# A decoder trunk in split fp32r: the block form at pairs 5, 7 to 19, and a scheduler told of a longer load latency

## The chip, the core and the metric

The kernel runs on one core of one Trainium2 chip. The metric is the device time of one execution in microseconds; the median of three runs counts. Times inside an execution are microseconds from the start of the profiled span. TensorE's matmuls are called PE, its weight loads PEld, VectorE DVE, ScalarE ACT, GpSimd POOL; SP issues most of the loads.

## What is computed

Two layers over 512 tokens of width 1024, then a final norm. Cut to what matters:

```python
for l in range(DEPTH):                                   # DEPTH = 2
    mod = silu(c) @ w_ada[l] + b_ada[l]
    sh1, sc1, g1, sh2, sc2, g2 = split(mod, 6)
    h = modulate(rmsnorm(x, norm1[l]), sh1, sc1)
    proj = h @ w_in[l]                                   # retention, gates and pooling branches
    ...
    x = x + g1 * (merged @ w_out[l])
    h2 = modulate(rmsnorm(x, norm2[l]), sh2, sc2)
    gate, up = split(h2 @ w_ffn_in[l], 2)                # 1024 x 5632: 22 pairs of 128 columns
    x = x + g2 * ((silu(gate) * up) @ w_ffn_out[l])      # 2816 x 1024
return rmsnorm(x, final_norm)
```

## The kernel before

**Split products.** Every weight and activation tile is split into a rounded part (hi) and a rest (lo), both fp32r. A product is three matmuls: hi·hi, lo·hi, hi·lo (mm3). Activations lie transposed, as 8 tiles (k-tiles) of 128 features by 512 tokens.

**Weights.** They stream in chunks of 8 blocks of 128x128 (512 KB, tensor wst). For a chunk, prep loads it into one of three raw tiles (SP), rounds it to hi (a cast, on ACT or DVE) and makes lo by a subtraction (DVE or POOL). For chunks for which is_added says so, ACT writes -hi into lo instead, and a DMA issued by POOL adds the weights to it from memory. Eleven w tiles hold hi and lo. ahead() prepares a chunk and the two behind it (LOOK). The three raw tiles also take the rows of w_ada, 96 loads in all: each is multiplied with silu(c) and summed by one DVE instruction (mod_tile).

**The FFN.** A pair i is a tile of gate columns and one of up columns, so 16 weight blocks, two chunks. In the plain form each is 8 k-tiles times 3 matmuls of 512 columns, 48 a pair; then SiLU on ACT, a product on DVE, and a split (cast and subtraction). In the block form (seven) the two tiles, the two halves of k and the two halves of the tokens are a 2x2 product of blocks done with seven products instead of eight: 7 products times 4 k-tiles times 3 matmuls, 84 matmuls of 256 columns. It needs sums of the activations (sums, the x tiles, made once a layer), sums of its weights (four instructions of 256 columns for each chunk, more casts and subtractions, seven_prep), four PSUM banks instead of two, and five additions on DVE behind the matmuls before SiLU. A block's two chunks are also prepared in the plain form by ahead() of the plain pair before it; nothing reads those. SEVEN (line 66) lists the pairs that are done as blocks: 4, 6, ... 20 in both layers.

The FFN runs in two halves, pairs 0 to 10 and 11 to 21 (FF_CUTS); behind each, ffn_out multiplies the hidden tiles and adds the result to x (close). The first ffn_out of a layer starts with output tile 0, over hidden tiles 0 to 10 in order, so pair 10's is read last. The first two pairs are partly made by first_tiles, and the sums are made while pairs 1 to 3 run.

**What sets the order.** All work is recorded first (Recorder). PE executes in program order. The other engines' order is set by a list scheduler (order) with costs of its own: each operation has a due time, counted back from the matmul that needs it, and LATENCY (line 217) of the engine is added from an operation's end to what depends on it. For "sync", the loads by SP, it is 1.6 us behind the cost of the transfer. It enters the due times, the moment at which a load's readers count as ready, and the moment at which buffers come free. The scheduler also chooses between ACT and DVE or DVE and POOL for some operations, by which would be done sooner.

**The start.** For each of the 8 k-tiles, two rows of w_ada and one chunk of w_in are loaded into the three raw tiles, the modulated k-tile of h is made, and 24 matmuls are issued into eight banks (start). Loads of the rotary tables (x from rot) stand in SP's queue between them.

In the trace nearly every instruction has line 421, that of the call which emits it (below: emit); so one goes by tiles: h are activations, x sums (and other pairs of tiles), w weights, r rows kept (hidden tiles, sums of weights), t temporaries, ps PSUM banks, xall the residual stream.

Of the kernel before, what the change touches and what calls it, by code (L numbers as in the profile page):

```python
# [17 lines left out]
DEPTH = 2  # L18
# [8 lines left out]
FT = FF // P  # L27
# [35 lines left out]
STAT_TILES = {"out": 4, "ffn_out": 3}  # L63
STAT_AT = 2

SEVEN = [set(range(4, FT, 2)), set(range(4, FT, 2))]
HALF_KT = KT // 2


# [144 lines left out]
TABLES = (AF.Sigmoid, AF.Silu, AF.Abs_reciprocal_sqrt)  # L214
TABLE_US = 1.28
LANDS = 6.0
LATENCY = {"tensor": 0.19, "vector": 0.05, "scalar": 0.05, "gpsimd": 0.05, "sync": 1.6}


class Recorder:  # L220
    def __init__(self):
        self.ops, self.tags, self.urgent = [], {}, False
        for e in LATENCY:
            setattr(self, e, Engine(self, (e,)))
# [28 lines left out]
    def deadlines(self):  # L253
# [13 lines left out]
        for op in reversed(self.ops):  # L267
# [3 lines left out]
            for o in op.after + reuse.get(op, []):  # L271
                if o.n > op.n:
                    op.due = min(op.due, o.due - LATENCY[e] - op.cost(e) - (LANDS if op.added else 0.0))
            if op.urgent and (e == "sync" or op.table is AF.Silu):
                op.due = op.n - 1e6

    def order(self):
# [4 lines left out]
        self.deadlines()  # L282
        free = {e: 0.7 for e in LATENCY}
        free["sync"] = 1.7
# [10 lines left out]
        taken, warm, late = set(), 6.83, 0.0  # L295
        ready = {e: [] for e in LATENCY}
        pe = [o for o in self.ops if o.engines[0] == "tensor"]
        pe_at = 0

        def arrive(o):  # L300
            pe = o.engines[0] == "tensor"
            o.at = max([done[b] + (0.0 if pe and b.ran == "tensor" else LATENCY[b.ran]) for b in o.before] or [0.0])
            for e in o.engines:
# [22 lines left out]
        while len(out) < len(self.ops):  # L326
            best = None
            for e in LATENCY:
                if e == "tensor":
# [103 lines left out]
def trunk(ctx, tc, xT, cin, wada, vecs, wst, rot, trid, icnt, out):  # L433
# [424 lines left out]
    for l in range(DEPTH):  # L858
# [222 lines left out]
        for f, (i0, i1) in enumerate(zip(FF_CUTS, FF_CUTS[1:])):  # L1081
            hid = []
            for i in range(i0, i1):
                if i in SEVEN[l]:
                    hid.append(seven(i))
# [114 lines left out]
```

## Time and profile before

| | |
|---|---|
| runs, us | 1560.45, 1557.97, 1560.12; median 1560.12 |
| the profiled execution, us | 1553.07, its span 1551.3 |
| mean granted TensorE clock in it | 0.992 |
| POOL's DMAs (w from wst) | 129 of 512 KB, 7.6 us median from issue to landing |
| SP's loads of w_ada (raw from wada) | 96 of 512 KB, 4.9 us median |

The profiled execution is a run of its own: its parts are compared with its own span. A row of the page's groups gives line, engine, operation, out<-in with partitions x elements and the count, then busy time, mean ns of one, and the engine's idle time ahead of them. A row of a timeline gives start and duration in us, engine, line, operation, operands, count, and in brackets the engine's idle time just before, with the instruction that ended it. A row of the windows gives the stretch, its length, busy time and count of PE, PEld, DVE, ACT and POOL, and then the granted clock, the share of DMA and GB/s.

### The profile page before, as it was taken

What the parts mean: (1) busy time and instruction counts of PE and PEld (TensorE: products, weight loads), DVE (VectorE), ACT (ScalarE), POOL (GpSimd) and SP (SyncE); (2) the same over time, 40 slices, a digit from 0 to 9 for tenths busy, and PEclk for the clock granted to TensorE, in tenths of its full rate; (3) what the DMA queues carried; (4) which work ended last, traced back from release to release, by engine and by line L of the source; (5) the groups of instructions that cost most, each with busy time, mean ns of one, the idle gap of its engine ahead of it and who ended that gap; (6) DMA issues with size and microseconds to landing.
All of it is one profiled execution on the core that took longest, in us unless ns stands there. A gap on an engine that the chain in (4) does not pass through costs nothing. (4 is left out here: it accounts for less than half of the span.)

```text
span 1551.3 us, 20752 instructions
## 1 busy us (share of the span) xinstructions
PE 1507.6 (97%) x7950; PEld 1290.2 (83%) x7950; DVE 1022.4 (66%) x1677; ACT 669.8 (43%) x949; POOL 292.2 (19%) x279
## 2 busy tenths in 40 slices
PE   7999999999999999999999999999999999999997
PEld 5788878888888878998898888888889887889987
DVE  7887693366568866888376767435647887368833
ACT  2387552223455321343267766323227544234432
POOL 0023150011133310122011322211111513001101
PEclk9999999999999999999999999999999999999999
DMA  7758637789784486556687865768897646534553
GB/s 251 250 154 214 154 84 216 203 240 269 170 217 155 158 245 190 163 182 217 198 206 162 209 157 124 206 181 234 242 233 179 200 164 197 155 123 150 174 139 82
DMA packets 83367, 288.89 MB, mean 186 GB/s; under 512 B 9282, under 2 KB 11586, under 8 KB 83267
## 3 DMA queue, kind: packets, MB, share of 16 engines
q1 hardware_dynamic: 64690, 219.92, 42.6%
q0 software_dynamic: 18576, 67.64, 24.3%
q8 instruction: 62, 1.02, 0.3%
q14 instruction: 39, 0.31, 0.1%
HBM read 285.43 MB, written 2.10 MB: 185 GB/s over the span
## 5 line engine op out<-in xcount | busy, mean ns | idle before, releaser
L421 PE MATMUL ps<-h,w 128*128 128x512 f32 (+1 forms) x3864 | 781.7, 360 | 8.2 <-DVE h L421 4.4
L421 PEld LDWEIGHTS ps<-h,w 128*128 128x128 f32 x3864 | 650.6, 189 | 123.4 <-ACT h L421 4.8
L421 PE MATMUL ps<-r,w 128*128 128x512 f32 (+1 forms) x2430 | 479.9, 357 | 7.4 <-DVE r L421 4.5
L421 PEld LDWEIGHTS ps<-r,w 128*128 128x128 f32 x2430 | 402.8, 188 | 78.5 <-DVE r L421 6.7
L421 ACT CAST w<-raw 128x1024 fp32r<-128x1024 f32 (+2 forms) x192 | 194.5, 1014 | 350.9 <-DMA raw<-wst 228.0
L421 POOL DMA_DIRECT2D w<-wst x129 | 115.4, 894 | 734.9 <-ACT w L421 673.4
L421 DVE TENSOR_TENSOR w<-raw,w 128x1024 fp32r<-128x1024 f32 (+2 forms) x158 | 194.2, 1234 | 88.5 <-PE ps L421 45.1
L421 ACT ACTIVATE w<-w 128x1024 fp32r<-128x1024 f32 x129 | 136.6, 1059 | 176.9 <-PE ps L421 60.8
L421 DVE SCALAR_TENSOR_TENSOR raw<-raw,cact 128x1024 f32<-128x1024 f32 x96 | 123.9, 1293 | 121.6 <-DMA raw<-wada 116.0
L421 DVE CAST w<-raw 128x1024 fp32r<-128x1024 f32 (+2 forms) x108 | 77.4, 717 | 106.3 <-DMA raw<-wst 58.7
L421 PE MATMUL ps<-x,w 128*128 128x256 f32 x864 | 109.3, 281 | 8.0 <-DVE w L421 4.2
L421 PEld LDWEIGHTS ps<-x,w 128*128 128x128 f32 x864 | 104.5, 190 | 9.6 <-DVE w L421 5.1
L421 POOL TENSOR_TENSOR r<-t,r 128x512 fp32r<-128x512 f32 x41 | 67.5, 1655 | 157.5 <-ACT r L421 144.9
L421 ACT CAST r<-t 128x512 fp32r<-128x512 f32 (+1 forms) x114 | 69.9, 618 | 47.6 <-DVE t L421 40.9
L421 PE MATMUL ps<-w,h 128*128 128x512 f32 x384 | 90.3, 395 | 0.0
L421 PEld LDWEIGHTS ps<-w,h 128*128 128x128 f32 x384 | 72.0, 188 | 17.7 <-ACT r L421 0.3
L421 DVE SCALAR_TENSOR_TENSOR xall<-ps,mod,xall 128x512 f32<-128x512 f32 (+1 forms) x62 | 38.7, 629 | 65.9 <-PE ps L421 65.8
L421 ACT ACTIVATE t<-ps 128x512 f32<-128x512 f32 x74 | 43.7, 592 | 50.4 <-PE ps L421 50.3
L421 DVE TENSOR_TENSOR w<-r,w 128x512 fp32r<-128x512 f32 x70 | 51.1, 737 | 12.4 <-ACT w L421 5.5
L421 ACT ACTIVATE t<-xall 128x256 f32<-128x256 f32 (+1 forms) x46 | 22.3, 497 | 82.3 <-DVE xall L421 79.1
L421 DVE TENSOR_TENSOR t<-ps,t 128x512 f32<-128x512 f32 x78 | 53.2, 684 | 6.3 <-PE ps L421 5.0
L421 ACT COPY t<-ps 32x512 f32<-32x512 f32 (+2 forms) x90 | 48.0, 535 | 21.4 <-DVE t L421 11.9
(95 smaller groups left out, 1020.8 us busy)
## 6 DMA issues: line engine op xcount, KB each, us to landing
raw<-wst SPq DMA_DIRECT2D x299, 512.0 KB, 4.6
w<-wst POOLq DMA_DIRECT2D x129, 512.0 KB, 7.6
raw<-wada SPq DMA_DIRECT2D x96, 512.0 KB, 4.9
x<-rot SPq DMA_DIRECT2D x32, 256.0 KB, 7.5
xall<-xT SPq DMA_DIRECT2D x4, 512.0 KB, 6.1
out<-t SPq DMA_DIRECT2D x7, 256.0 KB, 2.3
out<-t SPq DMA_DIRECT2D x2, 128.0 KB, 2.0
tri<-trid SPq DMA_DIRECT2D x1, 128.0 KB
```

What stands on the lines that cost most here:

```text
L421: getattr(eng, method)(*[real(a) for a in args], **{k: real(v) for k, v in kw.items()})
```

## The change

Two numbers change. The block form is taken by pairs 5, 7, ... 19 of both layers, 8 each instead of 9: pairs 4, 6, ... 20 are plain now, and the odd ones from 5 to 19 are blocks. The latency of SP's loads, for the scheduler, is 2.6 us instead of 1.6.

```diff
-SEVEN = [set(range(4, FT, 2)), set(range(4, FT, 2))]
+SEVEN = [set(range(5, FT - 1, 2))] * DEPTH
...
-LATENCY = {"tensor": 0.19, "vector": 0.05, "scalar": 0.05, "gpsimd": 0.05, "sync": 1.6}
+LATENCY = {"tensor": 0.19, "vector": 0.05, "scalar": 0.05, "gpsimd": 0.05, "sync": 2.6}
```

PE's program order changes only by the pairs' forms. On the other engines the scheduler sets a new order, and three places of it are shown. The numbers in names only tell tiles of one build apart.

**First place: DVE in the start,** behind the rounding of h's second k-tile (h_271 before, h_250 now). raw from wada is multiplied with cact; raw_257 and raw_224 are the third chunk of w_in. Before:

```order
39 L421 TENSOR_SCALAR h_271<-t_260,mod_0_150 128x512
40 L421 SCALAR_TENSOR_TENSOR raw_204,mod_0_150<-raw_204,cact_73 128x1024
41 L421 CAST w_286<-raw_257 128x1024
42 L421 SCALAR_TENSOR_TENSOR h_291<-t_260,mod_0_150,h_271 128x512
43 L421 SCALAR_TENSOR_TENSOR raw_235,mod_0_150<-raw_235,cact_73 128x1024
```

Now:

```order
41 L421 TENSOR_SCALAR h_250<-t_236,mod_0_150 128x512
42 L421 CAST w_269<-raw_224 128x1024
43 L421 SCALAR_TENSOR_TENSOR raw_182,mod_0_150<-raw_182,cact_73 128x1024
44 L421 TENSOR_TENSOR w_288<-raw_224,w_269 128x1024
45 L421 SCALAR_TENSOR_TENSOR raw_194,mod_0_150<-raw_194,cact_73 128x1024
46 L421 SCALAR_TENSOR_TENSOR h_307<-t_236,mod_0_150,h_250 128x512
```

The cast of the chunk moved ahead of the product with the first of the two w_ada rows, and the lo part of h moved behind both products. On SP, four loads of rotary tables stand right behind this chunk's load now, where one stood between the next two w_ada loads.

**Second place: ACT in layer 0's first FFN pairs.** ps_3511 is pair 0's gate tile and ps_3526 pair 1's; x tiles are the sums, r_3906, r_3901 and r_3980 sums of pair 4's weights. Before:

```order
280 L421 ACT_TABLE_LOAD
281 L421 ACTIVATE t_3930<-ps_3511 128x512
282 L421 CAST w_3915<-r_3901 128x512
283 L421 CAST w_3942<-raw_3870 128x768
284 L421 CAST r_3949<-t_3930 128x512
285 L421 CAST x_3973<-t_3889 128x512
286 L421 CAST w_3988<-r_3980 128x512
287 L421 CAST x_3996<-t_3928 128x512
288 L421 ACTIVATE t_4003<-ps_3526 128x512
```

Now:

```order
273 L421 ACT_TABLE_LOAD
274 L421 ACTIVATE t_3900<-ps_3511 128x512
275 L421 CAST x_3917<-t_3882 128x512
276 L421 CAST r_3921<-t_3900 128x512
277 L421 CAST x_3933<-t_3894 128x512
278 L421 ACTIVATE t_3946<-ps_3526 128x512
```

The casts of the block's weights are gone from between the two SiLUs (ACTIVATE t<-ps).

**Third place: the end of layer 0's first FFN half.** On ACT, t_4817 is the block at pair 10 before; raw tiles are chunks of the ffn_out that follows:

```order
336 L421 CAST r_4797<-t_4762 128x512
337 L421 CAST w_4806<-raw_4756 128x1024
338 L421 CAST w_4830<-raw_4781 128x1024
339 L421 ACTIVATE t_4817<-t_4817 128x512
340 L421 ACTIVATE w_4852<-w_4830 128x1024
```

On ACT now, t_4666 is the block at pair 9 and t_4732 the plain pair 10 (ps_4685 its gate tile):

```order
321 L421 ACTIVATE t_4666<-t_4666 128x512
322 L421 CAST w_4717<-raw_4670 128x1024
323 L421 ACTIVATE t_4732<-ps_4685 128x512
324 L421 CAST w_4741<-raw_4697 128x1024
325 L421 ACTIVATE w_4749<-w_4741 128x1024
```

And on DVE now, up to pair 10's split (raw_4738 is a row of layer 1's w_ada, ps_4730 pair 10's up tile):

```order
573 L421 SCALAR_TENSOR_TENSOR raw_4738,mod_0_4770<-raw_4738,cact_73 128x1024
574 L421 TENSOR_TENSOR t_4732<-ps_4730,t_4732 128x512
575 L421 CAST r_4785<-t_4732 128x512
576 L421 TENSOR_TENSOR r_4791<-t_4732,r_4785 128x512
```

Pair 10's SiLU now reads a bank directly and has one cast of a loaded chunk ahead of it instead of two.

## The prediction

> **What bounds the kernel.** First comes the first part of the page, the busy shares, and the last long piece of the chain of work that ended last.
>
> ```profile
> span 1551.3 us, 20752 instructions
> PE 1507.6 (97%) x7950; PEld 1290.2 (83%) x7950; DVE 1022.4 (66%) x1677; ACT 669.8 (43%) x949; POOL 292.2 (19%) x279
> ...
> 1309.20 231.97 PE ps L421 x1312
> ```
>
> PE is busy for 1507.6 of 1551.3 us, and from 1309 us on the end hangs on an unbroken run of matmuls. So the time is PE's work plus the 43.7 us in which it stands still. What another engine saves counts only where PE waits for it. The second view is therefore PE's timeline, with its idle time in brackets; these are its twelve longest waits between 70 and 1500 us.
>
> ```profile
> 226.16 0.51 PE L421 MATMUL ps<-r,w 128*128 128x512 f32 x1 [1.81 <-DVE r L421]
> 228.14 1.52 PE L421 MATMUL ps<-r,w 128*128 128x512 f32 x3 [1.47 <-ACT r L421]
> ...
> 426.38 0.99 PE L421 MATMUL ps<-acc,ones 128*128 128x256 f32 x2 [2.02 <-DVE acc L421]
> ...
> 474.21 4.62 PE L421 MATMUL ps<-x,w 128*128 128x256 f32 x24 [2.96 <-ACT t L421]
> ...
> 545.79 0.86 PE L421 MATMUL ps<-x,w 128*128 128x256 f32 x5 [1.02 <-DVE w L421]
> ...
> 556.89 55.16 PE L421 MATMUL ps<-r,w 128*128 128x512 f32 x234 [2.65 <-DVE r L421]
> ...
> 792.51 0.70 PE L421 MATMUL ps<-acc,ones 128*128 128x256 f32 x2 [1.95 <-DVE acc L421]
> ...
> 1232.17 0.50 PE L421 MATMUL ps<-x,w 128*128 128x256 f32 x2 [0.57 <-DVE x L421]
> 1233.87 0.85 PE L421 MATMUL ps<-x,w 128*128 128x256 f32 x5 [1.20 <-DVE w L421]
> ...
> 1255.37 0.39 PE L421 MATMUL ps<-x,w 128*128 128x256 f32 x1 [0.36 <-ACT w L421]
> ...
> 1295.52 0.85 PE L421 MATMUL ps<-x,w 128*128 128x256 f32 x5 [1.61 <-DVE w L421]
> ...
> 1309.20 54.98 PE L421 MATMUL ps<-r,w 128*128 128x512 f32 x239 [1.43 <-DMA w<-wst]
> ```
>
> They sum to 19.05 us. Eight of the twelve, 11.80 us, lie in a block form or right behind one (w with x as the two operands occurs in block forms alone; 556.89 and 1309.20 are the first ffn_out, behind pair 10). All of those belong to the first half of a layer's FFN; behind the second half's five blocks there is none. The third view is the windows, for the granted clock (PEclk, the last column but two), in the 3.4 us behind four of these waits.
>
> ```profile
> 228.70:232.10 3.40, 3.40 (x9) 2.56 (x9) 2.01 (x5) 1.39 (x2) 0.89 (x1) 0.50 0.47 152
> ...
> 474.40:477.80 3.40, 3.40 (x17) 3.40 (x17) 3.40 (x6) 2.50 (x5) 1.79 (x2) 0.51 0.00 0
> 556.40:559.80 3.40, 2.90 (x7) 2.28 (x8) 3.35 (x7) 0.00 (x0) 0.88 (x1) 0.50 0.92 225
> 792.50:795.90 3.40, 3.38 (x27) 3.33 (x28) 2.75 (x7) 0.47 (x1) 0.00 (x0) 1.00 1.06 276
> ```
>
> A wait has a second price: after 2.96 and 2.65 us of idle time the clock was halved for 3.4 us, so half of PE's busy time there was lost, 1.70 and 1.45 us; after 1.95 us it was not.
>
> **Two blocks fewer.** A pair in block form is 84 matmuls of 256 columns; in the plain form it is 48 of 512.
>
> ```profile
> 644.74 2.88 PE L421 MATMUL ps<-x,w 128*128 128x256 f32 x24
> 647.46 2.20 PE L421 MATMUL ps<-h,w 128*128 128x256 f32 x18
> 649.50 2.88 PE L421 MATMUL ps<-x,w 128*128 128x256 f32 x24
> 652.22 13.19 PE L421 MATMUL ps<-h,w 128*128 128x256 f32 x66
> 665.25 2.88 PE L421 MATMUL ps<-x,w 128*128 128x256 f32 x24
> ...
> 1376.42 2.99 PE L421 MATMUL ps<-x,w 128*128 128x256 f32 x24
> 1379.24 2.28 PE L421 MATMUL ps<-h,w 128*128 128x256 f32 x18
> ```
>
> From start to start, layer 0's block takes 2.72 + 2.04 + 2.72 + 2.04 = 9.52 us (the other 18 h products merge into the rows of 66). The 48 wide matmuls in that row take 13.03 - 2.04 = 10.99. So a block saves 1.47 us. In layer 1, 24 short matmuls take 2.82 us instead of 2.72, 84 take 9.87, and a block saves 1.12. One block fewer per layer: 1.47 + 1.12 = **+2.6 us**, all of it on PE and so on the path. If every block ran at either pace it would be 2.2 or 2.9.
>
> **Pair 4 of layer 0 becomes plain.** The wait at 474.21 is for the bank that pair 1's SiLU on ACT frees.
>
> ```profile
> 473.56 0.59 ACT L421 ACTIVATE t<-ps 128x512 f32<-128x512 f32 x1
> ```
>
> That SiLU stands (second place of the order above) behind pair 0's with six casts between them, five of them for the block's weights and sums; now it is three, two of them for sums. The first block starts with pair 5, 10.99 us later, which covers 2.96 four times. I take the wait and its half clock as gone: 2.96 + 1.70 = **-4.7 us**. The ends are -4.7 and 0 (the wait comes again at pair 5).
>
> **Pair 10 becomes plain.** Its weights cost 1.02 us at 545.79, its result 2.65 at 556.89.
>
> ```profile
> 547.20 7.05 PE L421 MATMUL ps<-r,w 128*128 128x512 f32 x30
> ...
> 552.33 1.05 ACT L421 CAST w<-raw 128x1024 fp32r<-128x1024 f32 x1 [4.73 <-DMA raw<-wst]
> ...
> 554.54 0.63 ACT L421 ACTIVATE t<-t 128x512 f32<-128x512 f32 x1
> ...
> L421 DVE TENSOR_TENSOR t<-ps,t 128x512 f32<-128x512 f32 x78 | 53.2, 684 | 6.3 <-PE ps L421 5.0 <-ACT t L421 0.9
> ...
> L421 DVE TENSOR_TENSOR r<-t,r 128x512 fp32r<-128x512 f32 x51 | 35.9, 708 | 2.7 <-ACT r L421 1.8
> ...
> L421 DVE CAST r<-t 128x512 fp32r<-128x512 f32 x26 | 11.1, 425 | 1.4 <-POOL t L421 0.7
> ```
>
> The first 30 matmuls of ffn_out don't need pair 10, which hides 6.9 us behind it. The block's SiLU came at 554.54, since ACT is in order and stood 4.73 us at a cast for a load. A plain pair's SiLU is of its first tile, and can run while PE makes the second; behind the second only a product, a cast and a difference are left, 0.68 + 0.43 + 0.71 = 1.8 us on DVE. Ahead of them on DVE stands a product of a late adaLN load (raw_4738, third place), so the load has 5.1 us of room. All three prices go: 1.02 + 2.65 + 1.45 = **-5.1 us**; ends -5.1 and, if that load is the next late thing, -1.0.
>
> **Layer 1.** The five waits at 1232 to 1309 sum to 5.17 us, without half clocks. The blocks at 4, 6 and 10 are plain now, and so is what stands ahead of the close at 1309; the block at 5 is new, and may bring back as much as the shortest, 0.57. So I take the others as gone: 1.20 + 0.36 + 1.61 + 1.43 = **-4.6 us**, ends 0 and -5.2.
>
> **Nothing for the rest of the blocks.** Each switch from plain to block also prepares the two next chunks in the plain form that the block then loads anew: 299 loads of wst stand in the row below against 263 chunks, 36 = 2 x 18; 295 remain. They go from engines with room, and cost or gain nothing while PE doesn't wait there.
>
> **The longer latency.** The scheduler plans with it, so it moves orders. The largest move is in the first 70 us (first place).
>
> ```profile
> 26.70 1.22 DVE L421 SCALAR_TENSOR_TENSOR raw<-raw,cact 128x1024 f32<-128x1024 f32 x1
> ...
> 29.03 0.69 DVE L421 CAST w<-raw 128x1024 fp32r<-128x1024 f32 x1 [1.10 <-DMA raw<-wst]
> ...
> 41.89 5.78 PE L421 MATMUL ps<-h,w 128*128 128x512 f32 x24 [1.71 <-DVE h L421]
> 48.61 11.24 PE L421 MATMUL ps<-h,w 128*128 128x512 f32 x48 [0.94 <-DVE h L421]
> 60.55 11.27 PE L421 MATMUL ps<-h,w 128*128 128x512 f32 x48 [0.70 <-ACT h L421]
> ...
> raw<-wst SPq DMA_DIRECT2D x299, 512.0 KB, 4.6
> ...
> L421 DVE SCALAR_TENSOR_TENSOR raw<-raw,cact 128x1024 f32<-128x1024 f32 x96 | 123.9, 1293 | 121.6 <-DMA raw<-wada 116.0 <-issue 5.4
> ```
>
> The start runs on three raw buffers: a load of 4.6 us, a use on DVE, the next load into the same buffer. PE waits for h three times there, so this chain decides, not PE. Before, DVE did the product at 26.70 (1.29 us) while it waited for the load of the cast at 29.03. Now the cast stands ahead of the product, so the product no longer fills that wait: DVE falls behind by 1.29. The cast's load itself is about 1 us later, an estimate: one addition and one product more (1.29) now stand on DVE ahead of the subtraction that frees its buffer, and I take half of their time as hidden in DVE's waits for loads. Together 2.3 us. The buffer that the product frees is later still: cast to 30.7, product to 32.0, against 27.9, so 4.1. If DVE has to wait for the load that follows there, the chain loses up to that. PE's first tile may start as much later, but PE has room for that in its later waits for h, as long as the chain is the slower of the two. Between 2.3 and 4.1, nearer to what is sure, I take **+2.8 us**; ends 0 (loads land earlier than the median) and +4.1.
>
> At 226 us two waits and a half clock (1.70) cost 5.0. In the new order the last head's pooled sums move ahead of its norm on DVE, and the head before gives its difference to POOL: one for, one against. Bounds 0 and -5.0; I take **-1.0**, near the unchanged end. The waits at 426 and 792 stay: the same accumulations stand in the same order.
>
> **The sum.** 2.6 - 4.7 - 5.1 - 4.6 + 2.8 - 1.0 = -10.0 us. The profiled execution took 1553.07 (span 1551.3), so 1543.1; the runs' median is 1560.12, 1.0045 times as much. By that ratio the forecast is **1550.0 us**.
>
> **A page's rule.** The row first: 2.65 us of idle time was followed by half clock. The Trainium skill, TensorE: Matmul & The Clock Gate, in the section Why this matters for your kernels, asks for no gaps over about 3 us between bursts. By it, waits of 2.96 and 2.65 would not halve the clock, and their removal would bring only themselves, a sum of -6.9 instead of -10.0; the trace disagrees with it at 474 and 556.
>
> **The rivals.** *All falls:* the 226 waits go whole (-4.0 more), the start keeps its time (-2.8), and layer 1's eight blocks run at layer 0's pace (8 x 0.35 = -2.8): -19.6, 1540.4 us. For it: a 256-column matmul seems to go slower behind a wait (layer 1's blocks follow five). Against: each needs its own luck. *Layer 1 keeps its waits:* -5.4, so 1554.7. For it: the 1.61 and 1.43 are late weights and loads, and block 5's weights are subtracted on DVE too. *The clock halves anyway:* the half windows are not due to the waits removed, and 3.15 us stay: -6.9, 1553.2. Against it: 792.50 at full clock. *The waits move with the block (slower):* the first block always finds sums, banks and weights late, wherever it stands, and pair 9 hands on what pair 10 did. Then only +2.6 + 2.8 = +5.4 is left: 1565.5 us. It decides if DVE and ACT are more than 10.99 us behind at pair 4; 2.96 speaks against that. That nothing changes is excluded, as PE has 72 matmuls fewer.
>
> **Chances.** Forecast 0.56, all falls 0.13, layer 1 waits 0.17, clock 0.04, moved waits 0.10. A measurement of this kernel can tell about 0.2% from no change, 3.1 us. Faster: 0.56 + 0.13 + two thirds of 0.17 + 0.03 = 0.83; same 0.08; slower 0.09. The range reaches from all falls to past the layer 1 case, with the bounds of the start and of the 226 waits: 1540 to 1558; it leaves the moved waits out.
>
> **What would show it.** The plain pair 4 without a wait at its start and pair 5 with under 1 us; no wait of ffn_out for pair 10's r; no half clock at 474 or 556; the second stage (w as weights' input, at 71.70 before) starting near 74.5; 16 blocks at 113 or 118 ns a matmul. The forecast is wrong if PE waits over 2 us at pair 5, or if the start costs more than 4.1.

## The result, and the profile after

| | before | after |
|---|---|---|
| runs of the first comparison, median, us | 1559.05 (1549.15 to 1560.45, 4 runs) | 1535.49 (1531.60 to 1537.89, 4 runs) |
| ratio of the times | | 0.986 (95% interval 0.9814 to 0.9906) |
| the profiled execution, us | 1553.07, span 1551.3 | 1535.18, span 1533.0 |
| mean granted TensorE clock in it | 0.992 | 0.995 |

Faster by 1.4%. The forecast was 1550.0 us with a range from 1540 to 1558: the direction was right, but the time lies below the range. Two more timings of the same kernel gave 0.986 (0.9838 to 0.9881) and 0.9854 (0.9821 to 0.9887). Over all comparisons below, before has a median of 1555.5 in 50 runs, after 1534.5 in 14.

First the busy shares of the page of after:

```profile
span 1533.0 us, 20526 instructions
PE 1503.3 (98%) x7878; PEld 1287.2 (84%) x7878; DVE 1006.4 (66%) x1650; ACT 645.7 (42%) x912; POOL 300.5 (20%) x291
```

The span is 18.3 us shorter. PE is busy 4.3 us less, although two blocks fewer are 2.6 us more work, and it stands still 29.7 us instead of 43.7. PE's timeline of after, with the idle time in brackets; past 70 us these are all its waits over 1 us, and the one of 0.80 beside them:

```profile
22.02 30.37 PE L421 MATMUL ps<-h,w 128*128 128x256 f32 x144 [5.25 <-DVE h L421]
...
71.48 2.83 PE L421 MATMUL ps<-w,h 128*128 128x512 f32 x11
...
420.57 0.70 PE L421 MATMUL ps<-acc,ones 128*128 128x256 f32 x2 [2.29 <-DVE acc L421]
...
777.89 0.50 PE L421 MATMUL ps<-h,w 128*128 128x256 f32 x2 [1.35 <-DMA w<-wst]
...
1250.58 0.86 PE L421 MATMUL ps<-x,w 128*128 128x256 f32 x5 [0.80 <-DVE w L421]
...
1273.03 0.86 PE L421 MATMUL ps<-x,w 128*128 128x256 f32 x5 [1.28 <-DVE w L421]
```

The waits at pair 4, at pair 10 and at the first ffn_out of layer 0 are gone, and so are both at 226 us. Those at the two norms (426 and 792 before) stay, and two of layer 1's are left. The second stage starts at 71.48, not at 74.5.

Since the order of matmuls changes only in the forms of the pairs, the time between the same two matmuls can be set side by side. These lengths are worked out from the starts in PE's timelines, in us, of one execution each; the two in the middle are the first two experiments:

| stretch | before | blocks only | latency only | after |
|---|---|---|---|---|
| up to the second stage | 71.70 | 73.43 | 72.68 | 71.48 |
| retention of layer 0, to 216 us | 145.15 | 144.27 | 144.29 | 144.23 |
| the last head and pooled sums, 216 to 236 us | 19.33 | 20.00 | 14.12 | 14.13 |
| to the norm ahead of layer 0's FFN | 184.57 | 188.24 | 185.24 | 185.10 |
| layer 0's FFN, up to the first ffn_out | 126.45 | 122.58 | 122.21 | 121.09 |
| layer 0's FFN, the rest | 231.76 | 229.12 | 230.43 | 229.20 |
| layer 1 up to its FFN | 399.26 | 398.96 | 400.43 | 398.59 |
| layer 1's FFN, up to the first ffn_out | 123.65 | 119.28 | 122.07 | 121.61 |
| layer 1's FFN, the rest | 240.69 | 238.97 | 237.74 | 238.97 |

From before to after the four FFN rows lose 11.7 us, the row at 216 us loses 5.2, the retention 0.9; the start loses 0.2. With the +0.5 and -0.7 of the two rows in between these are the 18.2 us in all. One execution is not the kernel, though: over all profiles below that have the old order in the FFNs (five) or that of after (four), the four FFN rows sum to 722.6 to 725.9 us and to 706.4 to 710.9, so they lose 14.9 in the mean. The row at 216 us takes 17.05 to 20.00 (mean 18.87, five profiles) in the old order and 14.10 to 14.13 in the new (seven).

### The profile page after: what moved, and what is told of

The parts are those of the page before. It is cut to its first block, busy times and chain, and to the rows that moved or that the text cites. A ratio compares the mean times of both kernels' runs of the same rounds, so it can differ in the third digit from the quotient of the medians.

```text
span 1533.0 us, 20526 instructions
## 1 busy us (share of the span) xinstructions
PE 1503.3 (98%) x7878; PEld 1287.2 (84%) x7878; DVE 1006.4 (66%) x1650; ACT 645.7 (42%) x912; POOL 300.5 (20%) x291
## 5 line engine op out<-in xcount | busy, mean ns | idle before, releaser
L421 PE MATMUL ps<-h,w 128*128 128x512 f32 (+1 forms) x3888 | 793.4, 362 | 8.6 <-DVE h L421 5.2
L421 PEld LDWEIGHTS ps<-h,w 128*128 128x128 f32 x3888 | 659.1, 189 | 126.2 <-DVE h L421 6.4
L421 ACT CAST w<-raw 128x1024 fp32r<-128x1024 f32 (+2 forms) x181 | 183.3, 1013 | 346.9 <-DMA raw<-wst 190.3
L421 DVE TENSOR_TENSOR w<-raw,w 128x1024 fp32r<-128x1024 f32 (+2 forms) x162 | 206.4, 1276 | 102.5 <-PE ps L421 71.7
L421 PE MATMUL ps<-x,w 128*128 128x256 f32 x768 | 96.2, 280 | 2.1 <-DVE w L421 2.1
L421 PEld LDWEIGHTS ps<-x,w 128*128 128x128 f32 x768 | 92.8, 188 | 2.5 <-DVE w L421 2.5
L421 POOL TENSOR_TENSOR r<-t,r 128x512 fp32r<-128x512 f32 x48 | 79.8, 1669 | 41.1 <-ACT r L421 29.4
L421 ACT CAST r<-t 128x512 fp32r<-128x512 f32 (+1 forms) x106 | 65.2, 618 | 33.7 <-DVE t L421 25.7
L421 PE MATMUL ps<-x,r 128*128 128x256 f32 (+2 forms) x256 | 52.7, 323 | 0.0
```

Of the source, the lines that this page charges most:

```text
L421: getattr(eng, method)(*[real(a) for a in args], **{k: real(v) for k, v in kw.items()})
```

## The experiments

**The two halves of the change, each alone,** and both kernels profiled a second time. One number is changed back:

```diff
-LATENCY = {"tensor": 0.19, "vector": 0.05, "scalar": 0.05, "gpsimd": 0.05, "sync": 2.6}
+LATENCY = {"tensor": 0.19, "vector": 0.05, "scalar": 0.05, "gpsimd": 0.05, "sync": 1.6}
```

> The blocks at 5, 7 to 19 with the old latency of 1.6; everything ahead of the first FFN stands in the order of before. Theory (two separate gains): the FFN's gain belongs to the blocks and comes whole, the start and the waits at 226 us stay as before. From the two profiles layer 0's FFN shrank by 7.9 us and layer 1's by 3.8, so about 11.7 us under before, ratio 0.9925 (0.990 to 0.995); the waits at 226 us and their half clock are there, those at the first block and at the first ffn_out are not. Rival (the latency cured the FFN's waits): the waits at the first blocks and at ffn_out are still there, and with two blocks fewer it is 2.6 us slower than before, ratio 1.0017. Rival (the two only work together): within 2 us of before.

Measured: 0.9895 (0.9873 to 0.9918), some 16 us, a little more than was expected from the one pair of profiles, and near the 14.9 of the mean. PE's timeline of this run:

```profile
227.01 0.59 PE L421 MATMUL ps<-r,w 128*128 128x512 f32 x1 [1.81 <-DVE r L421]
228.99 1.65 PE L421 MATMUL ps<-r,w 128*128 128x512 f32 x3 [1.39 <-ACT r L421]
...
548.52 11.84 PE L421 MATMUL ps<-r,w 128*128 128x512 f32 x51
...
1278.53 0.86 PE L421 MATMUL ps<-x,w 128*128 128x256 f32 x5 [0.47 <-DVE w L421]
```

The waits at 226 us are there as before; the first ffn_out (548.52) starts without a wait, and layer 1 keeps 0.47 of its 5.17 us. The four FFN rows of the table lose 12.6 us. So the whole gain of the FFNs comes with the blocks alone, as the theory had it; layer 1 even loses less to waits than in after.

```diff
-SEVEN = [set(range(5, FT - 1, 2))] * DEPTH
+SEVEN = [set(range(4, FT, 2)), set(range(4, FT, 2))]
```

> The latency of 2.6 with the old blocks at 4, 6 to 20; everything ahead of the first FFN stands in the order of after. Theory (two separate gains): the 6.3 us that after gained by 236 us come here too (start -0.2, -0.9 at 101 us, -5.2 at 226 us), the FFN's waits stay in kind, so ratio 0.996 (0.993 to 0.999). Rival (the latency cured the FFN's waits as well): 18 + 2.6 us under before, ratio 0.987. Rival of the prediction (the start costs 2.8 and the gain at 226 us was luck of one execution): about +2 us, ratio 1.001.

Measured: 0.9887 (0.9871 to 0.9904), some 17.6 us, where the theory allowed 0.993 at best. The gain at 226 us is there (14.12 us for that row), as expected. But the FFN rows lose 10.1 us too. The theory of two separate gains fell here: the longer latency also cures most of the FFN's waits, though the pairs are where they were. How, ACT's timeline shows. Latency only:

```profile
451.25 0.60 ACT L421 ACTIVATE t<-ps 128x512 f32<-128x512 f32 x1
456.01 0.84 ACT L421 CAST w<-raw 128x768 fp32r<-128x768 f32 x1 [4.17 <-DMA raw<-wst]
...
460.23 0.59 ACT L421 ACTIVATE t<-ps 128x512 f32<-128x512 f32 x1
```

Before:

```profile
460.96 0.84 ACT L421 CAST w<-raw 128x768 fp32r<-128x768 f32 x1 [3.89 <-DMA raw<-wst]
...
465.82 0.60 ACT L421 ACTIVATE t<-ps 128x512 f32<-128x512 f32 x1
```

The two ACTIVATEs are the SiLUs of pairs 0 and 1. Before, ACT stood 3.89 us at a cast for the block's load and came to pair 0's SiLU only behind it, at 465.82; pair 1's followed at 473.56 and held up PE. With the longer latency that cast counts as ready later, so the scheduler puts pair 0's SiLU ahead of it. Pair 1's ends at 460.8, and PE enters the block unhindered; it is the same wait that the plain pair 4 removes. That the casts' place is the cause is read from these orders; no run moved the SiLU alone. PE of latency only:

```profile
465.18 2.99 PE L421 MATMUL ps<-x,w 128*128 128x256 f32 x24
...
495.36 0.85 PE L421 MATMUL ps<-x,w 128*128 128x256 f32 x5 [1.48 <-DVE w L421]
...
546.34 13.82 PE L421 MATMUL ps<-r,w 128*128 128x512 f32 x58 [0.74 <-DVE r L421]
```

Pair 4 has no wait, and pair 10's result costs 0.74 instead of 2.65. The effects of 12.6 and 10.1 us overlap: together the FFNs lose 11.7, no more than by the blocks alone.

> The kernel of before, unchanged, profiled a second time. Theory: the waits at 226, 426, 474 and 556 us have the same size within 0.5 us, since the order sets them; a half clock follows a wait only where more than 1.8 us of idle time lie within one stretch of 3.41 us, so each of these may come or not, at 1.7 us each. Rival (the waits at 226 us were an accident of one execution): they are under 1 us in sum here.

Measured: 1551.64 us, 1.4 below the first profile. The waits have their places again: 0.66 + 1.83 at 226 us, 3.88 at pair 4, 1.44 and 1.60 at pair 10. So those at 226 us are no accident, though single ones moved by more than the 0.5 expected: by 1.15 us at 226 (0.66 for 1.81), 0.92 at pair 4, 1.05 at ffn_out. The half clocks came in part elsewhere: three past 70 us, at 470, 788 and 1306, none of them at 226 (below); the row at 216 us took 17.05.

> The changed kernel, unchanged, timed and profiled a second time. Theory: the same waits as in its first profile within 0.5 us, none at 226 us; ratio 0.986 again (0.983 to 0.989). Its 256-column matmuls may run at 113.3 or 117.8 ns in each FFN: if they run at 113.3 throughout, 3 us less for each layer. Rival (the first profile was a lucky execution): the start over 2 us later, or a wait at 226 us.

Measured: 0.986 (0.9838 to 0.9881); no wait at 226 us again. The start ended at 73.30 this time, 1.8 us later than in the first profile of after, a scatter that the start shows in all profiles (below).

**What was late at 226 us.** Before, the last head's norm on DVE was late. DVE of before, then POOL:

```profile
219.39 0.89 DVE L421 TENSOR_TENSOR r<-t,ic 128x2 f32<-128x2 f32 x1
220.31 2.34 DVE L421 TENSOR_TENSOR r<-r,t 128x2 f32<-128x2 f32 x1
222.57 1.87 DVE L421 SCALAR_TENSOR_TENSOR t<-t,t 128x512 f32<-128x512 f32 x1
224.36 1.75 DVE L421 TENSOR_TENSOR r<-t,r 128x512 fp32r<-128x512 f32 x1
```

```profile
220.22 2.41 POOL L421 TENSOR_TENSOR w<-raw,w 128x1024 fp32r<-128x1024 f32 x1
222.59 2.97 POOL L421 TENSOR_TENSOR r<-r,r 128x512 fp32r<-128x512 f32 x2
```

A subtraction of two columns took 2.34 us: as long as POOL's subtraction beside it, which ends at 222.63, when DVE's next one starts. The Trainium skill, SBUF — State Buffer, in the section SBUF: two separate sides, says that DVE and GpSimd share one pair of ports, and that where a DVE instruction has two inputs in SBUF and GpSimd reads SBUF too, whichever starts first holds the pair for its whole instruction; the rows agree. In after the two-column subtraction takes 0.16 us. The norm's next two, 1.87 and 1.75 us, run beside the two instructions that POOL has behind its subtraction (222.59). In after the scheduler gives POOL's subtraction (of chunk 33's weights) to DVE, behind the norm. So it was moved by hand, in before to DVE and in after to POOL (nc.gpsimd in the line below); but for a few instructions next to it, the order stays as it was.

```diff
-                nc.either.tensor_sub(out=lo[:, s_], in0=raw[:, s_], in1=hi[:, s_].bitcast(F32))
+                eng = nc.vector if c == 33 else nc.either
+                eng.tensor_sub(out=lo[:, s_], in0=raw[:, s_], in1=hi[:, s_].bitcast(F32))
```

> The kernel of before with one subtraction moved from POOL to DVE, that of the chunk of weights which POOL makes at 220.2 us (2.41 us there) while DVE's instructions beside it are stretched. The rest of the program is in the old order except for a few instructions of that place. Theory (this subtraction holds up the last head's norm on DVE, and through it PE): the two waits at 226 us (3.28 us) and their half clock (0 or 1.7 us) go, ratio 0.997 (0.995 to 0.998). Rival (the place of the pooled sums ahead of the norm on DVE is what makes it late): the waits stay over 2.5 us in sum, ratio 1.000.

Measured: 0.9979 (0.9966 to 0.9992), 3.3 us. DVE of this run, then PE:

```profile
218.44 0.89 DVE L421 TENSOR_TENSOR r<-t,ic 128x2 f32<-128x2 f32 x1
219.36 1.22 DVE L421 TENSOR_TENSOR r<-r,t 128x2 f32<-128x2 f32 x1
220.50 0.68 DVE L421 SCALAR_TENSOR_TENSOR t<-t,t 128x512 f32<-128x512 f32 x1
...
223.58 1.01 DVE L421 TENSOR_TENSOR r<-t,r 128x512 fp32r<-128x512 f32 x1 [0.69 <-ACT r L421]
```

```profile
224.65 0.50 PE L421 MATMUL ps<-r,w 128*128 128x512 f32 x1 [0.31 <-DVE r L421]
```

The pooled sums still stand ahead of the norm, yet of 3.28 us of waiting 0.31 is left, with no half clock at this place; the row at 216 us takes 14.58. So the rival is out: it was the subtraction on POOL, with what it put off on POOL into the norm, and not the order of the pooled sums.

> The changed kernel with the same chunk's subtraction forced back to POOL. Theory (the subtraction on POOL is the cause): waits of 2 us or more appear at the last head's split near 220 us, against 0 in two profiles of after; 2 to 5 us slower than after, ratio to before 0.988 (0.987 to 0.990). Rival (the order of the pooled sums is the cause): no wait over 0.5 us there, ratio as after's, 0.986.

Measured: 0.9877 (0.9846 to 0.9909). POOL, DVE and PE of this run:

```profile
221.04 2.84 POOL L421 TENSOR_TENSOR w<-raw,w 128x1024 fp32r<-128x1024 f32 x1
```

```profile
222.31 2.11 DVE L421 TENSOR_TENSOR r<-t,r 128x512 fp32r<-128x512 f32 x1 [0.69 <-ACT r L421]
```

```profile
224.48 0.50 PE L421 MATMUL ps<-r,w 128*128 128x512 f32 x1 [1.19 <-DVE r L421]
```

A wait appears, of 1.19 us instead of the 2 expected: here POOL's subtraction meets only the last instruction of the norm (2.11 us beside it, 1.02 in after without it). The profile bears the cause out; the time, whose interval holds after's 0.986, doesn't show it.

**The start alone.** For the loads of the start the scheduler is told 2.6, for all others 1.6, in the kernel of before. DVE, ACT and SP then stand in the start as in after, and from the second stage on as in before. It was run twice.

```diff
+def latency(e, o):
+    return o.loads if e == "sync" else LATENCY[e]
...
+        self.loads = 2.6
...
+        op.loads = self.loads
...
-                    op.due = min(op.due, o.due - LATENCY[e] - op.cost(e) - (LANDS if op.added else 0.0))
+                    op.due = min(op.due, o.due - latency(e, op) - op.cost(e) - (LANDS if op.added else 0.0))
...
+        nc.loads = 1.6
         nc.sync.dma_start(out=ic, in_=icnt)
```

> The kernel of before with the latency of 2.6 for the loads of the start alone: DVE, ACT and SP stand there as in after, and in the order of before from the second stage on. Theory (the new order loses 1.2 us at the fourth chunk and the next chunks give it back): the time from the issue of the second to that of the eighth chunk's load stays at 43 us (41.9 to 43.8 in six profiles of both orders), the first matmul comes some 3 us later, the second stage starts at 71.7 plus or minus 1.2, ratio 1.000 (0.998 to 1.002). Rival (the prediction's step: DVE's 1.29 us and 1 us more stay): second stage near 74.5, ratio 1.0018.

Measured: 1.0021 (1.0001 to 1.0041), second stage at 71.98: the time spoke for the prediction's step, the profile against it. Hence the repetition.

> The run with the start alone in the new order, repeated, since its time (1.0021, 1.0001 to 1.0041) and its profile (start as long as before) did not point the same way. Theory (the start costs under 1.4 us): second stage within 71.7 plus or minus 1.2, ratio 1.000 (0.998 to 1.002). Rival (the prediction's 2.8 us, hidden in the profiled execution by luck): second stage past 73.5 or ratio 1.0018 or more again, interval above 1.

Measured: 1.0000 (0.9982 to 1.0018), second stage at 71.82. All profiles together: with the old order of the start the second stage begins at 71.26 to 73.43 (mean 72.02, four profiles), with the new one at 70.86 to 74.07 (mean 72.40, ten). By the profiles the new order costs 0.4 us, within their scatter, not 2.8; the two timings, some 3.3 and 0 us, would not decide it by themselves. PE's first matmul with h does come later. Before it stood at 18.88:

```profile
18.88 4.98 PE L421 MATMUL ps<-h,w 128*128 128x256 f32 x40 [2.37 <-ACT h L421]
```

In after it stands at 22.02, behind DVE instead of ACT (the first line of its timeline above). The new order gives DVE two of ACT's four instructions on the residual stream (t<-xall) and three of its four roundings of h (h<-t,mod) in the start, moves that the prediction did not weigh. PE's later waits in the start take the 3.1 us up: they fall from 5.4 us to 1.8. For the chain of loads, SP's issues of the third to fifth chunk of weights are the place that the prediction followed. Before:

```profile
24.89 0.33 SPq L421 DMA_DIRECT2D raw<-wst  x1
...
32.77 0.33 SPq L421 DMA_DIRECT2D raw<-wst  x1
...
41.28 0.33 SPq L421 DMA_DIRECT2D raw<-wst  x1
```

After:

```profile
23.81 0.33 SPq L421 DMA_DIRECT2D raw<-wst  x1
...
32.85 0.33 SPq L421 DMA_DIRECT2D raw<-wst  x1
...
40.73 0.33 SPq L421 DMA_DIRECT2D raw<-wst  x1
```

From the third chunk to the fourth it was 7.88 us and is 9.04, which looks like the product's 1.3 us. But over all profiles this gap is 7.88 to 8.43 (mean 8.10, four) in the old order and 7.70 to 9.94 (mean 8.72, ten) in the new, and in the two profiles of the start alone it is 7.94 and 7.70. So in the mean 0.6 us are lost there, and from the fourth chunk to the fifth, 8.42 and 7.87 in the mean, they come back at once. From the second to the eighth chunk it was 43.21 and is 43.01 (from 17.96 and 16.83 to 61.17 and 59.84).

**A shorter latency for the FFNs.** With the same helper: 2.6 ahead of layer 0's first FFN, 1.6 from there on, with the new blocks.

```diff
+        self.loads = 2.6
...
+        nc.loads = 1.6
         mods_done(l, 40)
```

> The blocks at 5, 7 to 19; latency 2.6 for loads recorded ahead of layer 0's first FFN, 1.6 from there on, so that the first part stands as in after and the FFN as in the run with the blocks only. Theory (the parts add, stage by stage): the first part keeps after's gain at 226 us (5.2 us), the FFNs have e1's waits (0.5 us in layer 1 instead of 2.1), so 1 us under after, ratio to before 0.985 (0.983 to 0.987). Rival (the FFN needs the longer latency): waits of over 2 us in sum in the FFNs besides those at the norms, ratio 0.988 or more.

Measured: 0.989 (0.986 to 0.992), so no better than after. The row at 216 us takes 14.10 and layer 1's first half 119.47, as the theory had it; but two waits of 0.94 and 1.14 us stood in layer 0's FFN, which the run with the blocks only, with the same order there, did not have. Both the time and these 2.1 us of waits are what the rival named. Yet the four FFN rows sum to 707.7 us, within the 706.4 to 710.9 of the order of after, so the profile shows no loss by the shorter latency in the FFNs, and no gain either. This run does not decide between the two.

**The chunks that nobody reads.** They are no longer prepared:

```diff
...
-            else:
+            elif cc not in blocks:
                 prep(cc)
...
+        c0 = len(order) // UNITS - 3
+        for i in SEVEN[l]:
+            blocks.update((c0 + 2 * i + (11 if i > 10 else 0), c0 + 2 * i + 1 + (11 if i > 10 else 0)))
```

> The changed kernel without the chunks that are prepared in the plain form and then loaded anew by a block: 263 loads of wst instead of 295, with their casts and subtractions (or negative copies and POOL's adding DMAs). Theory (the prediction's step: these cost nothing, since other engines have room): ratio to before 0.986 (0.984 to 0.988), the two waits of layer 1's first half (0.8 and 1.3 us) stay within 0.5 us. Rival (they are what makes layer 1's block weights late): the two waits go, 2 us less, 0.9845 or lower.

> The changed kernel once more, beside the runs of this call on the same chip, as their yardstick: ratio to before 0.986 (0.983 to 0.989), start between 70.5 and 74, no wait over 0.5 us between 215 and 235 us.

Measured: 0.985 (0.9818 to 0.9882), and 0.9854 (0.9821 to 0.9887) for after beside it (second stage at 72.84, no wait at 226 us). The busy shares without those chunks:

```profile
PE 1503.4 (98%) x7878; PEld 1288.9 (84%) x7878; DVE 961.6 (63%) x1627; ACT 629.3 (41%) x901; POOL 255.2 (17%) x261
```

DVE is busy 45 us less than in after, POOL as much, ACT 16, and layer 1's block weights are no longer late (no wait in its first half), but the time is the same within what is measured, some 5 us either way. The rival's sign came: both waits went, and layer 1's first half takes 118.48 us, here and in the run below, against 120.45 to 121.61 in four profiles with the loads. So the loads seem to cost 2 to 3 us there; the step that put them at nothing is not confirmed, and the times can't settle it.

**Ten blocks.** On top of that:

```diff
-SEVEN = [set(range(5, FT - 1, 2))] * DEPTH
+SEVEN = [{5, 7, 9, 11, 12, 14, 15, 17, 18, 20}] * DEPTH
```

> The same without unread chunks, with ten blocks a layer: 5, 7, 9, 11, 12, 14, 15, 17, 18, 20, so two more blocks in the second half of each FFN, where no profile shows a wait. Theory (a block saves 1.1 to 1.5 us as long as sums and weights keep up): 4 blocks more, 4.5 to 5.9 us under the run without unread chunks, ratio to before 0.9825 (0.981 to 0.985). Rival (two blocks in a row ask more of DVE, ACT and PSUM than a plain pair between them gives time for): waits of over 5 us in sum at the second halves, ratio 0.987 or more.

Measured: 0.9829 (0.9797 to 0.9861), median 1529.83 us against 1533.51 of after on the same chip. In the profile the second parts of the FFNs take 226.94 and 236.71 us instead of 229.20 and 238.89 in the run before it: 4.4 us for four blocks, 1.1 each, and no wait between two blocks in a row. The gain is at the lower end of what was expected. It is the lowest median here, but its interval still overlaps with that of after.

## Why the prediction was wrong

The forecast was 14.5 us too high, and the steps that failed are the start, the size of the waits at 226 us, and the ratio to the runs. Step by step:

- **Two blocks fewer (+2.6), pair 4 (-4.7), pair 10 (-5.1), layer 1 (-4.6)**: -11.8 in sum; the FFN rows lose 11.7. So close a match is luck: over all profiles it is 14.9. The plain pair 4 and pair 5 have no wait, neither has ffn_out, and no half clock came there. Layer 1 kept 0.80 + 1.28 us of its waits, 1.5 more than allowed. (The list of before's twelve longest waits had left out 0.67 at 955.89 and 0.45 at 1258.34, the second one in layer 1; no term hangs on them.) That layer 0's blocks ran at 117.8 ns a matmul in this execution and at 113.3 in before cost some 3 us that the change didn't bring. The reasons held, with one correction: the plain pair is not the only cure, since the longer latency takes the SiLU out from behind the casts as well.
- **The start (+2.8)**: this step failed. It measured -0.2 between the two profiles and +0.4 over fourteen. The sum followed one instruction that moved, and took what DVE falls behind there as lost for good. At the fourth chunk 1.2 us were lost in this execution and 0.6 in the mean, and the next chunk gave that back. The load that was to come 1 us later (the third chunk's) was issued 6.98 us behind the second's, against 6.93. That PE would start later and make it up in its waits for h was right.
- **The waits at 226 us (-1.0)**: this step failed in its size. They went whole, 3.28 us and the half clock, -5.2; against the mean of five profiles it is -4.7, and the move of the one subtraction alone was worth 3.3 (1.2 to 5.3) in the runs. The cause was seen in neither of the two moves that were weighed, the pooled sums and the difference given to POOL, but in a third, POOL's subtraction given to DVE. The two-column instruction of 2.34 us stood in DVE's timeline of before and would have told.
- **Nothing for the rest, and the norms' waits stay**: right for the norms; 2.02 and 1.95 became 2.29 and 1.35 + 0.39. For the loads that nobody reads it is open: two profiles without them are 2 to 3 us shorter in layer 1.
- **The ratio to the runs (1.0045)**: this step failed too, and cost 6.9 us, about as much as the other two together. After's profiled execution stands at its runs' median (1535.18 and 1535.49). The three runs of before at 1558 to 1560 lie above its median of 1555.5 in 50 runs, so 4.6 of the 7.05 us came with the sample of three. For the rest, a run differs from another by the half clocks and the pace, which are no fixed share of the span. The mean granted clock of the 50 runs is 0.9910, against 0.992 and 0.993 in the two profiled ones: 2 to 3 us. After's 14 runs have 0.9939, as its profiles have (0.993 to 0.995). That the fewer waits are the reason is argued from the half clocks, not shown by a run.

Of the 14.5 us, 8 are terms (3.0 of the start, 4.2 at 226 us, 0.9 in the retention, which the second profile of before also lacks and which is scatter), the rest is the ratio. The rival in which all falls named 1540.4; it was the nearest, with two of its three reasons: the waits at 226 us go whole, and the start keeps its time. Its third, the faster pace in layer 1, didn't come. The rule of the Trainium skill that was weighed (TensorE: Matmul & The Clock Gate, Why this matters for your kernels: no gaps over about 3 us) would have kept the half clocks out of the sum; they went with the waits, as the trace said.

## What to carry to other kernels

When a scheduler is told another number, it also moves work between engines: list those moves at each wait, and look in the trace for short instructions that last as long as their neighbour on another engine. Follow a delay in a chain of loads through to the next stage's start before booking it. And do not stretch a profiled sum to the runs' median by a factor when the difference may be made of a small sample, or of waits that the change removes.

## What the hardware showed besides

**When the clock is halved.** In 14 profiles each halved stretch between 70 and 1500 us is one window of 3.41 us, or two, and their starts in one execution lie whole multiples of 3.413 us apart. What decides is PE's idle time within the window just ahead, not the length of a wait. The same wait at layer 0's norm (2.29 and 2.10 us) in two executions of after; the columns behind the stretch's length are busy times of PE, PEld, DVE, ACT and POOL, and the granted clock stands third from the end. First profile of after:

```profile
419.00:422.41 3.41, 1.84 (x14) 1.79 (x15) 2.63 (x7) 2.68 (x7) 0.00 (x0) 1.00 0.39 139
422.42:425.83 3.41, 3.41 (x32) 3.41 (x31) 3.31 (x9) 3.22 (x5) 1.58 (x2) 1.00 0.42 43
```

Second profile of after:

```profile
419.28:422.69 3.41, 1.31 (x9) 0.98 (x8) 2.99 (x9) 3.13 (x9) 0.00 (x0) 1.00 0.85 244
422.70:426.11 3.41, 3.41 (x16) 3.30 (x15) 2.50 (x8) 2.68 (x4) 0.88 (x1) 0.50 0.01 2
```

In the first the window's edge cuts the wait, 1.57 us of idle time fall into the window, and the next is at full clock; in the second 2.10 us fall into it, and half the clock is gone for 3.4 us. Between 70 and 1500 us, over all 14 profiles, every window with 1.78 us or more of idle time was followed by a halved one (20 of 20), none with 1.61 or less that was itself at full clock, and between these 3 of 5 (1.64 to 1.75 us; the 1.8 us expected ahead of the second profile of before was a little too high). That is about half a window. The wait of 1.95 us at 792 in before was cut by an edge as well: 1.31 us fell into the first window, and the clock stayed. The Trainium skill, TensorE: Matmul & The Clock Gate, in its table of states in Part 1, has the clock halve after an idle window of about 3.4 us; the window's length agrees, but half of it idle was enough. So a wait of 2 to 3 us costs itself, and by chance 1.7 us more. The two profiles of before have four and three halved windows between 70 and 1500 us, the three of after none, one and none.

**Two paces of the same matmul.** PE's timeline at the same block of layer 0's second half in two profiles of after. First:

```profile
602.82 2.99 PE L421 MATMUL ps<-x,w 128*128 128x256 f32 x24
605.65 13.28 PE L421 MATMUL ps<-h,w 128*128 128x256 f32 x66
```

Second:

```profile
604.80 2.88 PE L421 MATMUL ps<-x,w 128*128 128x256 f32 x24
607.52 13.19 PE L421 MATMUL ps<-h,w 128*128 128x256 f32 x66
```

24 matmuls of 256 columns take 2.83 us from start to start in the one and 2.72 in the other, 117.8 and 113.3 ns each, over hundreds of microseconds and at full clock. The program is the same, and both paces occur within one execution too (before: 113.3 in layer 0's second half, 117.8 in layer 1). It is worth 2.5 us in layer 0's second half alone (229.20 against 226.67). In the run with the blocks only, the 512-column matmuls ran at 233.3 instead of 228.9 ns from the waits at 229 us on to about 400 us, 3.7 us in all. What sets the pace stays open.
